# Dot products of the modulation moved from the pooling inputs to beside two merges of a mixer

## The chip, the cores and the metric

The kernel runs on one core of a Trainium2 chip. The metric is the device time of one execution in microseconds (us), as the median of several runs. A trace of one execution, the profiled one, gives the times of single instructions; they are counted from the start of its span.

## The reference

Two layers over x of 512 rows and 1024 columns. Each layer has a feed-forward network (FFN), a mixer of three branches, and a second FFN. Nine modulation vectors of a layer come from the vector c:

```python
c_act = jax.nn.silu(c)
for l in range(DEPTH):
    mod = (c_act @ w_ada[l] + b_ada[l]).reshape(B, N_MOD, D_MODEL)
    h = modulate(rms_norm(x, norm_gain[l, 0]), mod[:, 0], mod[:, 1])
    x = x + 0.5 * mod[:, 2][:, None, :] * swiglu(h, ...)
    h = modulate(rms_norm(x, norm_gain[l, 1]), mod[:, 3], mod[:, 4])
    x = x + mod[:, 5][:, None, :] * hybrid_mixer(h, ...)
    h = modulate(rms_norm(x, norm_gain[l, 2]), mod[:, 6], mod[:, 7])
    x = x + 0.5 * mod[:, 8][:, None, :] * swiglu(h, ...)
```

The mixer has attention branches a and c, and branch b, which takes trailing averages over 2, 4, 8 and 16 rows for four groups of 128 channels and maps each group by a 128x128 matrix. The three are merged:

```python
branch = jnp.einsum('bsnw,nwd->bsnd', ys, w_branch)
gates = jax.nn.sigmoid(g_lin.reshape(B, S, N_BRANCHES, D_MODEL))
merged = jnp.sum(gates * branch, axis=2)
return merged @ w_out
```

## The kernel before

Everything is held transposed, 128 channels by 512 rows, in float32. A float32 product is made of three TensorE matmuls of rounded parts: `hi` by `hi`, `lo` by `hi` and `hi` by `lo` (lines 119, 120 and 121). `wchunk` fetches a 512 KB piece of weights on SyncE's queue (L266) into one of two `raw` buffers, ScalarE copies its `whi` (L277), and VectorE subtracts it to give `wlo` (L279); there are three of each. Products collect in four PSUM buffers called `acc`.

**The dots.** `c_act @ w_ada` is done on VectorE: 144 dot products, one for each of 2 layers x 9 vectors x 8 blocks of 128. `mod_step` loads a 512 KB piece of `w_ada` (L203) into a buffer of the named tag and takes its product with `silc`, the spread-out `c_act`, with a sum per partition (L206); small instructions behind it make a scale (L215) or a half (L217). The first 16 are done at the start. The other 128 wait in `mod_queue`, in order of layer and vector. Each call of `wchunk` calls `side_work`, which adds `MOD_RATE` to a credit while `in_ffn` is set and the tag is `v2`, and takes a dot from the queue (`mod_pop`) for each whole credit. `mod_need(l, j)` takes at once all that are missing up to vector j. It is called ahead of each part's down products for the gate of that FFN, at the head of the last part's first half through `prefetch` for what the next sub-layer wants (`mod_need(l, 5)` ahead of a mixer), and before the mixer's `w_out` products. `v2` has 4 buffers, the tag `b` has 17.

**An FFN.** It goes through its hidden blocks in three parts. Each makes the gate and up products of some blocks, then the down products of these blocks in two halves of 512 output columns. In the down products `MOD_RATE` is 1.25; in gate and up it is 1.0 in part 0 and 0 in the others. The last part's two halves also start the next sub-layer: the tag is set to `raw` there, so that no dot is taken beside them other than by `mod_need`.

**A mixer.** Behind the attention of branch c, which carries the merge of branch a, `Mixer.run` loads `silc` again and the pooling matrices, and then writes out, in order:

- four pooling inputs by `pool_front`: a chunk of weights, 24 matmuls, a copy `u` on ScalarE (L1027), one to four window adds on GpSimd (L1033), three VectorE instructions for the difference (`hd` L1037, `ssum` L1039 and L1040) and a split (L384, L385). `pool_back`, put off by `later(60, ...)`, multiplies by the group's matrix (three matmuls) and makes `y` (L1050 on ScalarE, L1051 on VectorE);
- the merge of branch c: for each of 8 columns a gate (24 matmuls over a `w_ubg` chunk), a tanh (L1083), 12 matmuls by half a `w_branch` chunk, and `put_c` (L1142 on VectorE, an add on GpSimd at L1143);
- the merge of branch b in the same form, with a split of the finished column in `put_b`;
- the `w_out` products, with `residual_tail` (L434) for each column block.

In the mixer `in_ffn` is set from ahead of the pooling inputs to behind merge c, with tag `v2` and rate 1.0: 16 dots, 4 at the pooling inputs and 12 beside merge c.

A scheduler orders each engine's instructions by expected times, so the order on an engine is not that of the source line by line.

Of the kernel before, what the change touches and what calls it, by code (L numbers as in the profile page):

```python
# [15 lines left out]
F32 = mybir.dt.float32  # L16
# [6 lines left out]
P = 128  # L23
T = 512
D = 1024
# [15 lines left out]
def encoder_kernel(tc, xT, c, w_ada, b_ada, gains, w_gate, w_up, w_down, w_qkv, w_f, w_ubg,  # L41
# [16 lines left out]
    NB, NRAW = 17, 2  # L58

    def nm(s):  # L60
        uid[0] += 1
        return f"{s}_{uid[0]}"

    def st(shape, dt, tag, bufs):
        return sb.tile(shape, dt, tag=tag, bufs=bufs, name=nm(tag))
# [4 lines left out]
    def mmt(shape=(P, T)):  # L70
        return ps.tile(list(shape), F32, tag="mm", bufs=4, name=nm("mm"))
# [17 lines left out]
    class Task:  # L89
# [3 lines left out]
        def run(self):  # L93
            fn, self.fn = self.fn, None
            if fn is not None:
                fn()

    def later(delay, fn, group=None):
        t = Task(pe[0] + delay, fn, group)
        tasks.append(t)  # L100
        return t
# [85 lines left out]
    @contextlib.contextmanager  # L187
    def after(what):

        if what in last:  # L190
            with tc.issue_after(last[what]):
                yield
        else:
            yield
# [3 lines left out]
    apre = cp.tile([P, L, 3, KD], F32, name="apre")  # L198

    def mod_step(l, j, d, tag="raw"):  # L200
        raw = st([P, D], F32, tag, {"v2": 4, "raw": NRAW}[tag])
        with after("dma"):
            nc.sync.dma_start(raw, w_ada[l, j, d])  # L203
        m = modc[:, l, j, d:d + 1]
        with after("norm"):
            dot = nc.vector.tensor_tensor_reduce(out=raw, in0=raw, in1=silc[0], scale=1.0,  # L206
                                                 scalar=badac[:, l, j, d:d + 1], op0=ALU.mult, op1=ALU.add,
                                                 accum_out=m).ins
        s, kind = divmod(j, 3)
        if kind == 1:  # L210
            g = gainc[:, l, s, d:d + 1]
            if in_start[0]:
                nc.scalar.activation(apre[:, l, s, d:d + 1], m, AF.Identity, scale=g, bias=g)
                return dot
            return nc.vector.scalar_tensor_tensor(apre[:, l, s, d:d + 1], m, 1.0, g, op0=ALU.add, op1=ALU.mult).ins  # L215
        if kind == 2:
            nc.vector.tensor_scalar(m, m, 0.5, None, op0=ALU.mult)  # L217
# [6 lines left out]
    mod_tag = ["v2"]  # L224

    def mod_pop():
        if mod_ptr[0] < len(mod_queue):
            mod_step(*mod_queue[mod_ptr[0]], mod_tag[0])
            mod_ptr[0] += 1
# [5 lines left out]
    MOD_RATE = [1.0]  # L235
    in_ffn = [True]
# [14 lines left out]
    def side_work(side=True):  # L251
        if quiet[0] > 0:
            quiet[0] -= 1
            if quiet[0] == 0:
                gate.clear()
        elif side and in_ffn[0] and mod_tag[0] == "v2":
            mod_credit[0] += MOD_RATE[0]
            while mod_credit[0] >= 1.0:
                mod_credit[0] -= 1.0
                mod_pop()  # L260
# [301 lines left out]
    class Ffn:  # L562
# [32 lines left out]
        def run(self, nxt):  # L595
            l, s, ms = self.l, self.s, self.ms
            in_ffn[0] = True
            mod_tag[0] = "v2"
            parts = ((0, 6), (6, 8), (14, 8))
            for part, (f0, nf) in enumerate(parts):  # L600
                acts = []
                n = 0
                if part == 0 and self.norm is None:
                    acts = self.start()
                    n = 3
                    blocks = Blocks()
                elif part == 0:
                    g0, u0, g1 = self.pre
                    pg, pu, pg1 = mmt(), mmt(), mmt()
                    for hs in range(2):  # L610
                        self.norm.back(hs, acc if hs else mmt)
                        cols = slice(hs * HALF, (hs + 1) * HALF)
                        if hs == 0:
                            later(FRONT1, lambda: self.norm.front(1, acc))
                            later(BACK1, lambda: self.norm.back(1, acc))
                        for k in range(KD):
                            self.unit(pg, g0, cols, (k,))
                            self.unit(pu, u0, cols, (k,))
                        self.unit(pg1, g1, cols)
                    u1 = self.gate_up(1, 1)  # L620
                    acts.append(self.act(0, pg, pu))
                    pu1 = mmt()
                    self.unit(pu1, u1)
                    acts.append(self.act(1, pg1, pu1))
                    n = 2
                    blocks = Blocks(self.norm.xa, modc[:, l, 3 * ms])
                if part == 0:
                    blocks.schedule(T_FIRST, T_STEP)
                elif part == 1:
                    blocks.finish()  # L630
                MOD_RATE[0] = 0.0 if part else 1.0
                while part and n < nf:
                    both = [apply(p, AF.Silu)
                            for p in seven([w_gate[l, s, f0 + n + i] for i in range(2)], blocks, acc)]
                    ups = seven([w_up[l, s, f0 + n + i] for i in range(2)], blocks, mmt)
                    for i, sg in enumerate(both):
                        acts.append(self.act(n + i, None, ups[i], sg))
                    n += 2
                while n < nf:
                    g = self.gate_up(0, f0 + n)  # L640
                    u = self.gate_up(1, f0 + n)
                    pg, pu = mmt(), mmt()
                    self.unit(pg, g)
                    self.unit(pu, u)
                    acts.append(self.act(n, pg, pu))
                    n += 1
                mod_need(l, 3 * ms + 2)
                MOD_RATE[0] = 1.25
                for c0 in (0, T):
                    def src(c):  # L650
                        r0 = (f0 + 2 * c) * P
                        return w_down[l, s, r0:r0 + 2 * P, c0:c0 + T].rearrange("(k p) c -> p k c", p=P)

                    def ops(hi, lo, kt, j):
                        return (hi[:, j * P:(j + 1) * P], lo[:, j * P:(j + 1) * P],
                                acts[kt][:, 0, :], acts[kt][:, 1, :])

                    last = part == len(parts) - 1
                    if last and c0 == 0 and nxt is not None:
                        nxt.prefetch("v2")  # L660
                        mod_tag[0] = "raw"
                    split = last and c0 > 0
                    hook = None
                    if split:
                        hook = nxt.prefetch_weights if nxt is not None else (lambda: None)
                    for j, hs, o in k_outer(src, nf // 2, ops, hook):
                        d = c0 // P + j
                        residual_tail(d, hs, o, modc[:, l, 3 * ms + 2, d:d + 1], nxt if last else None)
                        if last and nxt is None:
                            cols = slice(0, T) if hs is None else slice(hs * HALF, (hs + 1) * HALF)  # L670
                            nc.sync.dma_start(out[:, d, cols], xd(d)[:, cols])
# [373 lines left out]
    def pool_back(l, g, b, wp, ys):  # L1045
        py = acc()
        triple(py, wp[0][:, g, :], wp[1][:, g, :], b[:, 0, :], b[:, 1, :], True, True)
        y = blk("b")
        sc = psc[:, l, g:g + 1]
        nc.scalar.activation(y[:, 0, :], py, AF.Identity, scale=sc)  # L1050
        nc.vector.scalar_tensor_tensor(y[:, 1, :], py, sc, y[:, 0, :].bitcast(F32), op0=ALU.mult, op1=ALU.subtract)  # L1051
        ys.append(y)
# [39 lines left out]
    def drain(*gens):  # L1092
        for it in gens:
            for _ in it:
                pass

    class Mixer:
# [10 lines left out]
        def run(self, nxt):  # L1108
# [53 lines left out]
            silc[0] = st([P, D], F32, "b", NB)  # L1162
            nc.sync.dma_start(silc[0], sil_dram.broadcast_to([P, D]))
            wp = wpool_load(l)
            in_ffn[0] = True
            mod_tag[0] = "v2"
            MOD_RATE[0] = 1.0
            mc = merge_units(l, 2, yc, put_c)
            for gi in range(4):
                b = pool_front(l, gi)  # L1170
                later(60, lambda gi=gi, b=b: pool_back(l, gi, b, wp, yb))
            drain(mc)
            in_ffn[0] = False
            poll(True)
            mb = merge_units(l, 1, yb, put_b)
            drain(mb)

            for b in range(4):
                xb = blk("xv", F32)
# [84 lines left out]
```

## Time and profile before

| what | value |
|---|---|
| median of 3 runs | 2412.22 us (2412.08 to 2413.41) |
| the profiled execution | 2411.93 us, its span 2410.1 us |
| its mean TensorE clock | 0.998 of full speed |
| TensorE (PE) busy | 98% |
| VectorE (DVE) busy | 72% |
| ScalarE (ACT) busy | 50% |
| GpSimd (POOL) busy | 15% |
| the dots, L206 | 144, 195.4 us in all |

In the rows of a timeline the first two numbers are the start and the length in us; then come engine, line, operation, output and inputs, and shapes. A bracket at the end gives the time for which the engine had been idle before it, and what ended that. The merge of branch c starts at about 682 us in layer 0 and 1874 us in layer 1; the last part of FFN 1 takes its first half of down products at about 320 to 340 us and 1510 to 1530 us.

### The profile page before, as it was taken

Reading aid. Unit: us, or ns where it says so; the run is one execution under the profiler, and the core shown is the slowest. Engines: PE = TensorE matmul, PEld = TensorE weight load, DVE = VectorE, ACT = ScalarE, POOL = GpSimd, SP = SyncE. Lnnn points to the kernel's source line nnn. Section 1 sums busy time; section 2 is a strip of 40 time slices with the busy share of each in tenths; the row PEclk is TensorE's granted clock in tenths of the full one; section 3 lists DMA queues with packets and bytes.
Section 4 is the critical chain, followed back from the end, with each engine's and each line's share of the span. In section 5 each row is a group of like instructions: output and inputs, shape, how many; then the busy total and the mean of one; then the engine's idle time right before and its main releaser. Section 6 shows DMA issues by size and latency. Waiting matters only on the chain. (4 is left out here: it accounts for less than half of the span.)

```text
span 2410.1 us, 36817 instructions
## 1 busy us (share of the span) xinstructions
PE 2363.2 (98%) x14106; PEld 2088.6 (87%) x14106; DVE 1729.5 (72%) x3070; ACT 1199.8 (50%) x2090; POOL 353.3 (15%) x423
## 2 busy tenths in 40 slices
PE   7999999999999999999999999999999999999999
PEld 5898998778878898989998989978787788989898
DVE  8987876787673377878577878677866734769583
ACT  5353545786632353535553636466865233536362
POOL 3000011144432110000000000102444322000000
PEclk9999999999999999999999999999999999999999
DMA  7635352323353425353325352523234533333233
GB/s 273 210 106 193 106 201 80 93 79 108 116 196 131 140 97 205 103 190 106 132 82 194 103 183 105 201 79 98 79 116 142 183 114 140 130 107 104 92 106 103
DMA packets 116437, 320.93 MB, mean 133 GB/s; under 512 B 11139, under 2 KB 13315, under 8 KB 116261
## 3 DMA queue, kind: packets, MB, share of 16 engines
q1 hardware_dynamic: 115106, 314.38, 38.6%
q0 software_dynamic: 1152, 4.19, 0.4%
q8 instruction: 111, 1.82, 0.3%
q14 instruction: 66, 0.53, 0.1%
q10 hardware_dynamic: 2, 0.00, 0.0%
HBM read 312.16 MB, written 6.38 MB: 132 GB/s over the span
## 5 line engine op out<-in xcount | busy, mean ns | idle before, releaser
L277 ACT CAST whi<-raw 128x1024 fp32r<-128x1024 f32 (+1 forms) x267 | 277.4, 1043 | 449.1 <-PE acc L120 258.6
L279 DVE TENSOR_TENSOR wlo<-raw,whi 128x1024 fp32r<-128x1024 f32 x259 | 323.5, 1252 | 208.4 <-ACT whi L277 205.7
L119 PE MATMUL acc<-b,whi 128*128 128x512 f32 (+1 forms) x960 | 360.6, 376 | 0.0
L120 PE MATMUL acc<-b,whi 128*128 128x512 f32 (+1 forms) x960 | 357.1, 372 | 0.0
L121 PE MATMUL acc<-b,wlo 128*128 128x512 f32 (+1 forms) x960 | 356.6, 371 | 0.0
L206 DVE CUSTOM_DVE_ANT_0 v<-v,b,badac 128x1024 f32<-128x1024 f32 x144 | 195.4, 1365 | 40.2 <-DMA v<-in_w_ada_dram 40.1
L119 PEld LDWEIGHTS acc<-b,whi 128*128 128x128 f32 x960 | 180.8, 188 | 31.4
L121 PEld LDWEIGHTS acc<-b,wlo 128*128 128x128 f32 x960 | 180.8, 188 | 31.3
L120 PEld LDWEIGHTS acc<-b,whi 128*128 128x128 f32 x960 | 180.9, 188 | 29.9
L121 PE MATMUL acc<-hhi,wlo 128*128 128x512 f32 x480 | 189.4, 395 | 7.9 <-DVE wlo L279 7.9
L119 PE MATMUL acc<-hhi,whi 128*128 128x512 f32 x480 | 192.2, 402 | 4.0 <-ACT whi L277 2.3
L120 PE MATMUL acc<-hlo,whi 128*128 128x512 f32 x480 | 189.5, 395 | 0.7 <-DVE hlo L711 0.7
L385 DVE TENSOR_TENSOR ptb<-v,ptb 128x1024 fp32r<-128x1024 f32 x128 | 156.6, 1224 | 35.7 <-ACT ptb L384 34.3
L384 ACT CAST ptb<-v 128x1024 fp32r<-128x1024 f32 x128 | 134.0, 1050 | 93.0 <-DVE v L452 46.4
L384 ACT CAST whi<-raw 128x1024 fp32r<-128x1024 f32 (+1 forms) x128 | 106.8, 834 | 97.9 <-PE acc L120 50.3
L119 PE MATMUL acc<-whi,hhi 128*128 128x512 f32 x336 | 137.8, 411 | 0.9 <-DVE xv L385 0.9
L121 PE MATMUL acc<-whi,hlo 128*128 128x512 f32 x336 | 132.0, 393 | 0.0
L120 PE MATMUL acc<-wlo,hhi 128*128 128x512 f32 x336 | 131.7, 392 | 0.0
L385 DVE TENSOR_TENSOR wlo<-raw,whi 128x1024 fp32r<-128x1024 f32 (+1 forms) x128 | 121.9, 952 | 7.0 <-ACT whi L384 5.2
L121 PEld LDWEIGHTS acc<-hhi,wlo 128*128 128x128 f32 x480 | 91.4, 190 | 29.0 <-DVE wlo L279 9.8
L434 DVE SCALAR_TENSOR_TENSOR xv<-acc,modc,xv 128x512 f32<-128x512 f32 (+1 forms) x112 | 76.9, 690 | 50.0 <-PE acc L121 50.0
L329 POOL TENSOR_TENSOR ssum<-ssum,t 128x256 f32<-128x256 f32 (+1 forms) x45 | 46.7, 1037 | 445.7 <-ACT t L328 445.6
(314 smaller groups left out, 6606.0 us busy)
## 6 DMA issues: line engine op xcount, KB each, us to landing
v<-in_w_ada_dram SPq DMA_DIRECT2D x144, 512.0 KB, 4.8
raw<-in_w_down_dram SPq DMA_DIRECT2D x88, 512.0 KB, 3.7
raw<-in_w_up_dram SPq DMA_DIRECT2D x82, 512.0 KB, 3.7
raw<-in_w_gate_dram SPq DMA_DIRECT2D x79, 512.0 KB, 3.7
raw<-in_w_ubg_dram SPq DMA_DIRECT2D x56, 512.0 KB, 3.5
raw<-in_w_qkv_dram SPq DMA_DIRECT2D x42, 512.0 KB, 3.9
raw<-in_w_branch_dram SPq DMA_DIRECT2D x24, 512.0 KB, 3.8
raw<-in_w_out_dram SPq DMA_DIRECT2D x16, 512.0 KB, 3.6
```

The source lines that it names most:

```text
L119: mm(o, lh, rh, start=start, stop=False)
L120: mm(o, lh, rl, start=False, stop=False)
L121: mm(o, ll, rh, start=False, stop=stop)
L206: dot = nc.vector.tensor_tensor_reduce(out=raw, in0=raw, in1=silc[0], scale=1.0, scalar=badac[:, l, j, d:d + 1], op0=ALU.mult, op1=ALU.add ...
L277: nc.scalar.copy(hi, raw)
L279: lo_eng.tensor_tensor(lo, raw, hi.bitcast(F32), op=ALU.subtract)
L329: nc.gpsimd.tensor_tensor(self.ssum[:, cols], self.ssum[:, cols], q, op=ALU.add)
L384: nc.scalar.copy(hi, src)
L385: nc.vector.tensor_tensor(lo, src, hi.bitcast(F32), op=ALU.subtract)
L434: nc.vector.scalar_tensor_tensor(x, acc_j, gate, x, op0=ALU.mult, op1=ALU.add)
```

## The change

The setting of `in_ffn`, tag and rate moves in `Mixer.run` from ahead of the pooling inputs to behind them, and it is taken back behind the merge of branch b instead of between the two merges. The tag in between is `b`, not `v2`, and for that `mod_step` learns the tag `b` and `side_work` lets every tag pass but `raw`. Behind the mixer the tag goes back to `raw`. The rate beside the down products falls from 1.25 to 1.0.

A mixer so takes 24 dots instead of 16: none at the pooling inputs, 12 beside merge c, and 12 at merge b, of which 8 are spread over its columns and 4 stand next to the start of `w_out`. The number of all dots stays 144; fewer are left for the down products.

```diff
     def mod_step(l, j, d, tag="raw"):
-        raw = st([P, D], F32, tag, {"v2": 4, "raw": NRAW}[tag])
+        raw = st([P, D], F32, tag, {"v2": 4, "raw": NRAW, "b": NB}[tag])
...
-        elif side and in_ffn[0] and mod_tag[0] == "v2":
+        elif side and in_ffn[0] and mod_tag[0] != "raw":
             mod_credit[0] += MOD_RATE[0]
...
                 mod_need(l, 3 * ms + 2)
-                MOD_RATE[0] = 1.25
+                MOD_RATE[0] = 1.0
...
             wp = wpool_load(l)
-            in_ffn[0] = True
-            mod_tag[0] = "v2"
-            MOD_RATE[0] = 1.0
             mc = merge_units(l, 2, yc, put_c)
             for gi in range(4):
                 b = pool_front(l, gi)
                 later(60, lambda gi=gi, b=b: pool_back(l, gi, b, wp, yb))
+            in_ffn[0], mod_tag[0], MOD_RATE[0] = True, "b", 1.0
             drain(mc)
-            in_ffn[0] = False
             poll(True)
             mb = merge_units(l, 1, yb, put_b)
             drain(mb)
+            in_ffn[0], mod_tag[0] = False, "raw"
```

## The prediction

> **What bounds the kernel now.** I read the page's engine line first, then the table by stretches around the pooling inputs, then the timelines of TensorE and of its feeders there.
>
> ```profile
> PE 2363.2 (98%) x14106; PEld 2088.6 (87%) x14106; DVE 1729.5 (72%) x3070; ACT 1199.8 (50%) x2090; POOL 353.3 (15%) x423
> ```
>
> PE is busy 2363.2 of 2410.1 us, so the change can pay only where PE stands still or runs slowly. The table by stretches (span, then busy time and count of PE, PEld, DVE, ACT, POOL, then granted clock, DMA share, GB/s) has two such places, the same one in each layer:
>
> ```profile
> 682.00:686.50 4.50, 0.55 (x4) 0.13 (x2) 3.55 (x7) 1.10 (x2) 2.64 (x6) 0.86 0.60 233
> 686.50:692.00 5.50, 5.50 (x13) 4.34 (x14) 5.50 (x6) 1.64 (x3) 4.26 (x4) 0.50 0.54 191
> 692.00:700.00 8.00, 8.00 (x36) 6.55 (x36) 7.49 (x14) 2.65 (x4) 2.86 (x3) 0.99 0.41 135
> 1878.70:1884.00 5.30, 5.28 (x16) 4.19 (x17) 5.30 (x6) 1.67 (x3) 4.04 (x4) 0.68 0.60 198
> ```
>
> A PE that looks full from 686.5 to 692 starts 13 matmuls where the next stretch starts 36 in 8.00 us. TensorE's timeline names the cause:
>
> ```profile
> 660.15 0.63 PE L966 MATMUL mm<-ident,t 128*128 128x128 f32 x4 [1.29 <-DVE t L954]
> ...
> 660.85 0.39 PE L121 MATMUL acc<-hhi,wlo 128*128 128x512 f32 x1
> ...
> 682.16 0.39 PE L120 MATMUL acc<-hlo,whi 128*128 128x512 f32 x1
> 686.50 0.80 PE L121 MATMUL acc<-hhi,wlo 128*128 128x512 f32 x1 [3.95 <-DVE wlo L279]
> ...
> 692.16 0.40 PE L119 MATMUL acc<-hhi,whi 128*128 128x512 f32 x1
> ...
> 698.36 0.39 PE L119 MATMUL acc<-hhi,whi 128*128 128x512 f32 x1
> ...
> 1874.43 0.39 PE L120 MATMUL acc<-hlo,whi 128*128 128x512 f32 x1
> 1878.72 0.50 PE L121 MATMUL acc<-hhi,wlo 128*128 128x512 f32 x1 [3.91 <-DVE wlo L279]
> ```
>
> Gate 0 of the merge of branch c has its `whi`, but waits 3.95 and 3.91 us for its `wlo`. Then the clock is down. In layer 0 it is 0.50, and 13 matmuls need 692.16 - 686.50 = 5.66 us; at 8.00/36 = 0.222 us each they would take 2.9, so 2.8 are lost. In layer 1 (clock 0.68) 16 matmuls fill 5.30 us, which is worth 1.7. The two places cost 3.95 + 2.8 + 3.91 + 1.7 = **12.4 us**, the most that the pooling part can give.
>
> Beside it stands a rule of the Trainium skill, page "TensorE: Matmul & The Clock Gate", section "Part 1: The HAM clock gate": an idle window of about 3.4 us halves the clock, and about 3.4 us of activity restore it. The trace agrees: the gaps of 3.95 and 3.91 us were followed by clocks of 0.50 and 0.68, the 1.29 us gap at 660.15 by a matmul of 0.39 us, as long as any at full speed, and 5.66 us passed before full speed came back. By that rule a remaining wait under 3.4 us costs its own length alone.
>
> **Pooling inputs.** Dots stand ahead of that `wlo` on DVE; these are the last three, and what else is in its queue:
>
> ```profile
> 674.94 2.06 DVE L206 CUSTOM_DVE_ANT_0 v<-v,b,badac 128x1024 f32<-128x1024 f32 x1
> ...
> 677.69 1.27 DVE L206 CUSTOM_DVE_ANT_0 v<-v,b,badac 128x1024 f32<-128x1024 f32 x1
> ...
> 681.48 2.06 DVE L206 CUSTOM_DVE_ANT_0 v<-v,b,badac 128x1024 f32<-128x1024 f32 x1
> ...
> 684.46 0.18 DVE L1037 TENSOR_TENSOR hd<-strip,icnt 128x16 f32<-128x16 f32 x1 [0.92 <-POOL strip L1033]
> ...
> 685.23 1.22 DVE L279 TENSOR_TENSOR wlo<-raw,whi 128x1024 fp32r<-128x1024 f32 x1
> ...
> 693.70 0.74 DVE L1051 SCALAR_TENSOR_TENSOR b<-acc,psc,b 128x512 fp32r<-128x512 f32 x1
> ```
>
> The change takes them out, and in the changed kernel's order this `wlo` also stands ahead of the third input's `hd`, `ssum` chain. So the last three dots (2.06 + 1.27 + 2.06 = 5.39) and the wait of 0.92 go: ready at 685.23 + 1.22 - 6.31 = 680.1, where PE wants it at 682.4. This wait is cured with 2 us to spare, without counting the earlier ones.
>
> What is late next? Gate 1's first matmul (698.36 now, 698.36 - 3.95 - 2.8 = 691.6 without the stall) needs the PSUM buffer of the second pool product, which `y1`'s L1051 (693.70 now) releases. In the new order that L1051 stands behind the fourth input's `hd` chain, and so behind POOL's four window adds. POOL and the ACT copies that start it:
>
> ```profile
> 678.38 0.58 ACT L1027 COPY b<-acc 128x512 f32<-128x512 f32 x1
> ...
> 686.87 0.58 ACT L1027 COPY b<-acc 128x512 f32<-128x512 f32 x1
> ...
> 679.04 1.43 POOL L1033 TENSOR_TENSOR strip<-b 128x512 f32<-128x512 f32 x1 [1.19 <-ACT b L1027]
> ...
> 680.55 1.90 POOL L1033 TENSOR_TENSOR strip<-strip 128x512 f32<-128x512 f32 x1
> ...
> 682.58 1.85 POOL L1033 TENSOR_TENSOR strip<-strip 128x512 f32<-128x512 f32 x1
> ...
> 687.60 1.13 POOL L1033 TENSOR_TENSOR strip<-b 128x512 f32<-128x512 f32 x1 [2.16 <-ACT b L1027]
> ...
> 692.81 2.11 POOL L1033 TENSOR_TENSOR strip<-strip 128x512 f32<-128x512 f32 x1
> ```
>
> The fourth copy (686.87) comes behind the third input's chain. That is shorter by its adds, 684.43 - 679.04 = 5.39 against three at 1.13, so 2.0, and by the dot of 2.06 that held the second input's `hd`, less about 1.05 for gate 0's `whi`, which moves ahead of the third copy: some 3.0 together. So the copy ends at 684.4; the four adds take 694.92 - 687.60 = 7.3 as traced beside dots, 4 x 1.13 = 4.5 alone; the `hd` chain 685.23 - 684.46 = 0.8 and L1051 0.74 follow. End: 690.4 to 693.3 against 691.6, a wait of 0 to 1.7. In the new order two dots still stand ahead of that chain, so I take 1.3. If the copy gains 0.8 only, it is 3.9. **Gain 12.4 - 2 x 1.3 = 9.8 us**, bounds 12.4 and about 4.
>
> **Down products.** With 1.0 for 1.25 they carry fewer dots, so that the forced batch ahead of the last half of part 2 of FFN 1 (`mod_need(l, 5)`) grows from 7 to some 10. Its loads pass the weights on SP's queue:
>
> ```profile
> 318.64 12.40 SPq L203 DMA_DIRECT2D v<-in_w_ada_dram  x7
> 331.15 0.89 SPq L266 DMA_DIRECT2D raw<-in_w_down_dram  x2
> ...
> 337.52 1.05 ACT L277 CAST whi<-raw 128x1024 fp32r<-128x1024 f32 x1 [4.90 <-DMA raw<-in_w_down_dram]
> ...
> 334.46 1.27 DVE L206 CUSTOM_DVE_ANT_0 v<-v,b,badac 128x1024 f32<-128x1024 f32 x1
> ...
> 338.60 1.23 DVE L279 TENSOR_TENSOR wlo<-raw,whi 128x1024 fp32r<-128x1024 f32 x1 [1.58 <-ACT whi L277]
> ...
> 340.26 0.39 PE L119 MATMUL acc<-b,whi 128*128 128x512 f32 x1
> ```
>
> Four `v2` buffers hold the loads back to the pace of the dots. Three more put the first weight's issue behind the end of the fifth dot, the one ahead of 334.46, so at about 334.3 instead of 331.15. Where it was cast 6.4 us after issue, it lands 4.5 to 7 us after; `whi` (1.05) and `wlo` (1.23) follow at 341.1 to 343.6, where PE takes `whi` at 340.26 and `wlo` 0.5 later. Waits of 0.4 to 2.9, softened because the scheduler has put `whi` products of two accumulators ahead: I take 1.2 a layer, **2.4 us**, bounds 0 and 6. The lower rate gains nothing elsewhere, as PE has no idle time in the down products; FFN 2 of layer 1 loses its last 8 dots to the mixer for nothing.
>
> **Merges.** A merge with dots is traced: c, today.
>
> ```profile
> 715.38 0.42 SPq L203 DMA_DIRECT2D v<-in_w_ada_dram  x1
> ...
> 719.90 1.28 DVE L206 CUSTOM_DVE_ANT_0 v<-v,b,badac 128x1024 f32<-128x1024 f32 x1 [2.35 <-DMA v<-in_w_ada_dram]
> ...
> 720.82 1.05 ACT L277 CAST whi<-raw 128x1024 fp32r<-128x1024 f32 x1 [6.61 <-PE acc L120]
> ...
> 721.91 1.23 DVE L279 TENSOR_TENSOR wlo<-raw,whi 128x1024 fp32r<-128x1024 f32 x1 [0.51 <-ACT whi L277]
> ...
> 724.02 0.39 PE L121 MATMUL acc<-hhi,wlo 128*128 128x512 f32 x1
> ```
>
> Of every two columns one gate has a dot ahead of its `wlo`. This `wlo` ends at 723.14, 0.9 before PE wants it, and the dot ends 0.7 before the `wlo` starts: a load may take 4.5 + 0.7 + 0.9 = 6.1 us before PE waits. The table by line and tile gives all loads and dots:
>
> ```profile
> L206 DVE CUSTOM_DVE_ANT_0 v<-v,b,badac x144: 1269/1280/2630, 11.4 to 2113.0; 128x1024 f32<-128x1024 f32 x144
> DMA to landing us min/median/max: 3.4/4.8/8.1
> ```
>
> At the median 4.8 nothing waits, and the 8 spread dots beside merge b, like the 4 bunched next to `w_out`, are hidden by its columns (24 matmuls for the gate and 12 for the branch, at 0.222 us: 16 us per pair). Merge b has its own split on DVE and POOL adds that may stretch a dot to 2.06, which eats 0.8 of the 1.6 to spare. I take 0.5 us for both layers, bounds 0 and 24 (the first rival).
>
> Sum: 9.8 - 2.4 - 0.5 = 6.9. 2411.93 for the profiled execution, which stands 0.3 under the runs' median of 2412.22 and 1.8 over its span, gives **2405.0**.
>
> **Rivals.** *Slower:* loads of the dots land late in the merges. Twelve even gates (six a mixer) have a dot ahead; each costs landing time less 6.1. At 8.1, the longest traced, that is 12 x 2.0 = 24, so 2405.0 + 24 = 2429; from a mean landing of 6.8 on the change is slower than before. For it: up to three transfers of 128x1024 f32 per column of 8 us, and many loads issued in a row behind the pooling. Against it: the row above, at the same pace. *Same:* the wait moves to gate 1. If the fourth copy gains only 0.8, both layers wait 3.9 and lose the clock too (2.8, 1.7), and nothing is left of the 12.4: 2411.9 + 2.4 less 12.4 - 2 x 3.9 - 2.8 - 1.7 = 0.1, about 2414. For it: POOL's adds in a row and dots beside them. Beside it, the page "SBUF — State Buffer", section "Who interferes with whom", says that a DVE instruction with two SBUF inputs and a GpSimd one that reads SBUF exclude each other; the dots of 1.27 and 2.06 and the adds of 1.13 and 1.90 agree; by it the chain would keep its 7.3 wherever the two dots fall among the adds, and gate 1 would wait 1.7 rather than 1.3. *Better:* POOL runs its adds near 1.13 and the batch is covered by the `whi` products: 2411.9 - 12.4 = 2399.5.
>
> **How the numbers follow.** 0.2% (4.8 us) is about what a measurement tells from no change: 2407.4 to 2417.0 is "same". Forecast 0.46; better 0.11; wait at gate 1 or a batch of 3 us and more a layer 0.25; late loads 0.18. The forecast's own spread is 2401 to 2409; the top of it lies in "same", the bottom of the third case in "faster", which I set against each other. Faster 0.57, same 0.25, slower 0.18. The range reaches from 2399 to 2416.
>
> **What would show it.** Right: no gap over 2 us before gate 0's L121 at 682 and 1874, clock 1.0 there, gate 1's first L119 released by L1051 at most 2 us late, a gap near 1 us in the second half of part 2 of FFN 1, merge b without PE gaps. Wrong: PE gaps before even gates' L121 in the merges with DVE at `wlo` behind a dot that waited for its load; a clock under 1 behind gate 1; or gaps over 3 us near 340 and 1530.

## The result and the profile after

The changed kernel takes 2407.35 us (median of 11 runs, 2402.77 to 2410.06) against 2411.89 us (11 runs, 2410.91 to 2413.41). The ratio is 0.9978, 95% interval 0.9970 to 0.9987: a gain of 4.5 us. 2405.0 was forecast, with a range of 2399 to 2416. The profiled execution took 2409.17 us (span 2407.4), 2.8 less than that of before.

**Gate 0 no longer waits.** The table by stretches of the changed kernel, with the columns of before; the next rows follow from its TensorE and VectorE timelines and those of the two helpers:

```profile
682.00:686.50 4.50, 4.50 (x22) 3.69 (x21) 2.25 (x5) 2.01 (x3) 2.27 (x6) 1.00 0.92 350
692.00:700.00 8.00, 6.46 (x29) 4.96 (x28) 5.50 (x9) 2.65 (x4) 2.81 (x4) 1.00 0.12 33
```

```profile
695.72 0.49 PE L119 MATMUL acc<-hhi,whi 128*128 128x512 f32 x1 [1.54 <-DVE b L1051]
...
1884.45 0.51 PE L119 MATMUL acc<-hhi,whi 128*128 128x512 f32 x1 [1.57 <-DVE b L1051]
```

```profile
679.66 1.23 DVE L279 TENSOR_TENSOR wlo<-raw,whi 128x1024 fp32r<-128x1024 f32 x1 [0.26 <-ACT whi L277]
...
687.78 2.06 DVE L206 CUSTOM_DVE_ANT_0 b<-b,b,badac 128x1024 f32<-128x1024 f32 x1
...
689.77 2.05 DVE L206 CUSTOM_DVE_ANT_0 b<-b,b,badac 128x1024 f32<-128x1024 f32 x1
...
694.16 0.18 DVE L1037 TENSOR_TENSOR hd<-strip,icnt 128x16 f32<-128x16 f32 x1 [2.33 <-POOL strip L1033]
...
694.92 0.74 DVE L1051 SCALAR_TENSOR_TENSOR b<-acc,psc,b 128x512 fp32r<-128x512 f32 x1
```

```profile
686.51 0.57 ACT L1027 COPY b<-acc 128x512 f32<-128x512 f32 x1
...
687.23 1.53 POOL L1033 TENSOR_TENSOR strip<-b 128x512 f32<-128x512 f32 x1 [2.20 <-ACT b L1027]
...
692.84 1.28 POOL L1033 TENSOR_TENSOR strip<-strip 128x512 f32<-128x512 f32 x1
```

From 682.0 to 686.5, where 4 matmuls started, 22 do, at full clock. The `wlo` of gate 0 ends at 680.89. What is late next is what the prediction named: gate 1, released by `y1`'s L1051, which stands behind the fourth input's `hd`, which waits for POOL's fourth add (to 694.12), with two dots ahead of it. Gate 1 waits 1.54 and 1.57 us. The four adds took 694.12 - 687.23 = 6.9 us beside those dots, close to the 7.3 of before and far from the 4.5 that four adds of 1.13 would take.

**The forced batch costs more than was forecast.** SyncE, ScalarE and TensorE around the last part of FFN 1 in layer 0, then TensorE in layer 1:

```profile
318.10 15.54 SPq L203 DMA_DIRECT2D v<-in_w_ada_dram  x9
333.69 0.43 SPq L266 DMA_DIRECT2D raw<-in_w_down_dram  x1
335.18 0.33 SPq L203 DMA_DIRECT2D v<-in_w_ada_dram  x1
...
340.26 1.04 ACT L277 CAST whi<-raw 128x1024 fp32r<-128x1024 f32 x1 [8.25 <-DMA raw<-in_w_down_dram]
```

```profile
341.36 0.50 PE L119 MATMUL acc<-b,whi 128*128 128x512 f32 x1 [1.44 <-ACT whi L277]
...
342.62 0.50 PE L121 MATMUL acc<-b,wlo 128*128 128x512 f32 x1 [0.30 <-DVE wlo L279]
...
1529.63 0.50 PE L119 MATMUL acc<-b,whi 128*128 128x512 f32 x1 [2.33 <-ACT whi L277]
...
1530.89 0.74 PE L121 MATMUL acc<-b,wlo 128*128 128x512 f32 x1 [0.30 <-DVE wlo L279]
```

```profile
339.73:343.13 3.40, 1.66 (x6) 0.96 (x6) 2.44 (x6) 1.27 (x2) 0.00 (x0) 1.00 0.96 374
343.14:346.55 3.41, 3.41 (x9) 2.67 (x9) 3.19 (x5) 1.86 (x2) 0.00 (x0) 0.50 0.75 247
1527.56:1530.97 3.41, 1.04 (x4) 0.57 (x4) 2.40 (x6) 1.04 (x1) 0.00 (x0) 1.00 0.82 317
1530.98:1534.38 3.40, 3.40 (x8) 2.67 (x9) 3.37 (x5) 2.09 (x2) 0.00 (x0) 0.50 0.64 196
```

The weight that was issued at 331.15 now is at 333.69, behind nine loads of dots. PE waits 1.44 + 0.30 us in layer 0 and 2.33 + 0.30 in layer 1, and behind the wait, in both places, the granted clock is 0.50 for 3.41 us. PE is busy all through these stretches, so half of them is lost: 1.7 us more each.

**Merge b carries its dots for nothing.** Two stretches that lie within merge b, one in each layer, after and then before:

```profile
757.00:818.00 61.00, 61.00 (x271) 50.52 (x270) 32.72 (x48) 19.87 (x26) 12.47 (x8) 1.00 0.54 185
1946.00:2008.00 62.00, 62.00 (x275) 51.36 (x274) 33.53 (x48) 19.88 (x26) 12.62 (x8) 1.00 0.53 184
```

```profile
757.00:818.00 61.00, 61.00 (x271) 50.52 (x270) 23.60 (x26) 18.56 (x25) 14.34 (x8) 1.00 0.39 129
1946.00:2008.00 62.00, 62.00 (x275) 51.35 (x274) 24.37 (x26) 20.00 (x27) 14.50 (x8) 1.00 0.37 128
```

VectorE has 9.1 and 9.2 us more to do and the traffic rises from 129 to 185 GB/s in layer 0. TensorE stays full and has the same 271 and 275 matmuls. In merge c of layer 1 one gate waits 0.32 us for its `wlo` (at 1910.72), which it did not before. The longest load of a dot takes 6.6 us to land, against 8.1 before, and the median load 4.9 against 4.8:

```profile
DMA to landing us min/median/max: 3.4/4.9/6.6
```

### The profile page after: what moved, and what is told of

Same layout as the page of the kernel before. It is cut to its first block, busy times and chain, and to the rows that moved or that the text cites. A ratio compares the mean times of both kernels' runs of the same rounds, so it can differ in the third digit from the quotient of the medians.

```text
span 2407.4 us, 36815 instructions
## 1 busy us (share of the span) xinstructions
PE 2361.9 (98%) x14106; PEld 2086.8 (87%) x14106; DVE 1728.9 (72%) x3070; ACT 1197.8 (50%) x2090; POOL 351.7 (15%) x423
## 5 line engine op out<-in xcount | busy, mean ns | idle before, releaser
L206 DVE CUSTOM_DVE_ANT_0 v<-v,b,badac 128x1024 f32<-128x1024 f32 x96 | 127.2, 1333 | 12.3 <-DMA v<-in_w_ada_dram 12.0
L119 PEld LDWEIGHTS acc<-hhi,whi 128*128 128x128 f32 x480 | 90.7, 189 | 26.1 <-DVE b L1051 4.0
```

The source lines that it names most:

```text
L119: mm(o, lh, rh, start=start, stop=False)
```

## The experiments

Each ran beside the kernel before on one chip: e1 to e4 on one, e5 to e8 on a second, e9 and e10 on a third. The time of before there was 2411.86, 2413.03 and 2412.87 us, and gains are taken against these.

Gains by stage, below, come from the two profiled executions: the k-th matmul start of one trace is set against the k-th of the other (each has 14106, in almost the same order). From the pooling inputs into merge b (655 to 760 us of the kernel before, and 1848 to 1950) the changed kernel gains 4.8 and 3.7 us; in the last part of FFN 1 it loses 2.7 and 3.1; in the last FFN it loses 1.7.

**e1 to e4: where the gain comes from and where it goes.**

e1, the rate alone set back:

```diff
-                MOD_RATE[0] = 1.0
+                MOD_RATE[0] = 1.25
```

> The changed kernel with 1.25 instead of 1.0 beside the down products, so that the forced batch ahead of the last half of FFN 1 is 7 dots in layer 0 and 5 in layer 1 again; the mixer keeps its 24. Theory: the pooling part gains 10.3 us and the batch of 10 costs 5.8 (excess of PE over full pace 3.62 - 0.88 and 4.61 - 1.54). So 2411.9 - 10.3, about 2402, no PE gap over 1 us near 340 and 1525, and the 1.5 us gap at gate 1 stays. Rival, what is lost is lost to the dots beside merge b: the time stays at 2407.

2402.60 us, ratio 0.9968 (0.9956 to 0.9979). No gap near 340 and 1525 is left, and gate 1 waits as in the changed kernel:

```profile
693.05 0.50 PE L119 MATMUL acc<-hhi,whi 128*128 128x512 f32 x1 [1.57 <-DVE b L1051]
```

So with the old rate the change gains 9.3 us, and the lower rate takes half of it. The rival, dots beside merge b as the cost, falls. By stage, e1 gains 8.9 us from the pooling inputs into merge b and 3.0 in the last part of FFN 1, where layer 1 now forces five dots and before seven, and loses 1.7 in the last FFN.

e2, the kernel before with the rate alone changed:

```diff
-                MOD_RATE[0] = 1.25
+                MOD_RATE[0] = 1.0
```

> The kernel before with 1.0 for 1.25 alone: the forced batch is 9 dots, pooling inputs and merges as before. Theory: the batch costs 4 to 6 us, so 2416 to 2418, with gaps of 1 to 2.5 us in the last part of FFN 1 of both layers. Rival (the batch is covered, the loss lies in the mixer): 2412.

2415.82 us, ratio 1.0018 (1.0010 to 1.0027): 4.0 us slower by the rate alone. TensorE's timeline shows both the gap in the batch and the old one at gate 0:

```profile
341.39 0.50 PE L119 MATMUL acc<-b,whi 128*128 128x512 f32 x1 [1.43 <-ACT whi L277]
...
688.97 0.79 PE L121 MATMUL acc<-hhi,wlo 128*128 128x512 f32 x1 [3.94 <-DVE wlo L279]
...
1533.88 0.50 PE L119 MATMUL acc<-b,whi 128*128 128x512 f32 x1 [1.58 <-ACT whi L277]
```

e3, the changed kernel with a short batch:

```diff
         def prefetch(self, xtag):
-            mod_need(self.l, 5)
+            mod_need(self.l, 4)
```

> The changed kernel, but the prefetch of a mixer asks for its shift and scale alone (4 instead of 5): the forced batch is 2 dots, and the 8 of the mixer's gate come first among the dots beside its merges. Theory: without the batch the 5.8 us come back, 2407.4 - 5.8, about 2401.5, no PE gap near 340 and 1525. Rival (the batch costs nothing, or the dots that are now missing from FFN 1 cost as much elsewhere): 2407.

2400.87 us, ratio 0.9955 (0.9942 to 0.9967), 11.0 us under before and 6.5 under the change by the medians. TensorE is full in both places:

```profile
310.00:355.00 45.00, 45.00 (x293) 41.24 (x293) 30.72 (x43) 23.71 (x36) 6.24 (x5) 1.00 0.52 168
1500.00:1540.00 40.00, 40.00 (x251) 36.24 (x250) 24.78 (x33) 20.47 (x30) 6.08 (x5) 1.00 0.59 195
```

The mixer's gate needs its eight dots only ahead of `w_out`, and the 24 dots beside the merges deliver them in time. e1, e2 and e3 agree: the batch is the cost of the lower rate.

e4, the four pooling inputs in the other order, with `yb` still in the order of the groups:

```diff
-            for gi in range(4):
+            for gi in (3, 2, 1, 0):
...
-        ys.append(y)
+        ys.insert(0, y)
```

> The changed kernel with the four pooling inputs taken from the widest window to the narrowest, so that the last of them has one window add and not four. Theory: gate 1's wait of 1.55 and 1.57 us stands behind POOL's four adds (y1's L1051 is queued behind that chain on DVE), so it goes: 2407.4 - 3.1, about 2404.3. Rival A, the two dots ahead of that chain hold it by their loads: the gap stays, 2407. Rival B, the wide window now delays the first inputs and gate 0 waits again: 2409 or more.

2412.79 us, ratio 1.0004 (0.9995 to 1.0013). A miss: the gain is gone. The four adds at the start delay each later input, since each copy stands on ScalarE behind the split of the input ahead, and in the new order two dots stand between the last `hd` chain and `y1`'s L1051. VectorE and TensorE there:

```profile
691.69 1.28 DVE L206 CUSTOM_DVE_ANT_0 b<-b,b,badac 128x1024 f32<-128x1024 f32 x1
...
692.89 1.28 DVE L206 CUSTOM_DVE_ANT_0 b<-b,b,badac 128x1024 f32<-128x1024 f32 x1
...
694.70 0.74 DVE L1051 SCALAR_TENSOR_TENSOR b<-acc,psc,b 128x512 fp32r<-128x512 f32 x1
```

```profile
695.50 0.63 PE L119 MATMUL acc<-hhi,whi 128*128 128x512 f32 x1 [2.40 <-DVE b L1051]
```

Gate 1 waits 2.40, not 0, and in layer 0 the clock drops behind it. Neither rival was this: gate 0 waits only 0.31 in layer 0. The run says nothing for or against POOL's adds as the cause of gate 1's wait, since it put dots in their place.

**e7 and e8: gate 1's wait.** e7 is e3 with the pool products in another PSUM group:

```diff
     def pool_back(l, g, b, wp, ys):
-        py = acc()
+        py = mmt()
```

> The changed kernel with the short forced batch and the pool products (pool_back) in the other group of PSUM buffers, mm, so that gate 1 no longer needs the buffer that y1's L1051 releases. Theory: the gaps of 1.69 and 1.69 us at gate 1 go, 2400.9 - 3.4, about 2397.5. Rival (gate 1 is late for another reason that ends just ahead of it, its weights or the tanh of gate 0): the gap stays over 1 us, 2400.

2398.26 us, ratio 0.9944 (0.9930 to 0.9957). Gate 1 starts without a gap, on TensorE's timeline:

```profile
689.48 0.39 PE L119 MATMUL acc<-hhi,whi 128*128 128x512 f32 x1
...
716.07 0.50 PE L121 MATMUL acc<-hhi,wlo 128*128 128x512 f32 x1 [0.76 <-DVE wlo L279]
```

So it was the PSUM buffer, and the clock shows no loss there. A gap of 0.76 us appears at 716.07, in merge c, behind a dot whose load came late. The intervals of e3 and e7 overlap, and e7's profiled execution is not the faster one (2398.17 against 2397.79). The 2.4 us that it gains over e3 by stage, from the pooling inputs into merge b, it gives back in new waits behind, such as 0.76 us at 846.13. So e7 shows what gate 1 waited for, and not a faster kernel than e3.

e8 is e7 with 1.25 for 1.0:

> As the last one, with 1.25 for 1.0 beside the down products: no forced batch at all in FFN 1. Theory (the rate matters only through the batch): the same time as the last one, about 2397.5. Rival (1.25 itself crowds the down products): over 2 us slower.

2399.88 us, ratio 0.9942 (0.9930 to 0.9955), the same as e7: without the batch the rate does not matter. Both are faster than the kernel before and the changed kernel.

**e5, e9 and e10: the place or the buffer.** e5 moves the dots out of the pooling inputs and changes nothing else: the three settings stand behind the loop, with `v2` as before.

```diff
-            in_ffn[0] = True
-            mod_tag[0] = "v2"
-            MOD_RATE[0] = 1.0
...
+            in_ffn[0], mod_tag[0], MOD_RATE[0] = True, "v2", 1.0
             drain(mc)
```

> The kernel before with the dots taken out of the pooling inputs alone: 12 dots beside merge c, none beside merge b, 1.25 beside the down products; the 4 that are missing are forced beside w_out. Theory (the pooling part gains 10.3 us, dots beside merge b cost and gain nothing): 2411.9 - 10.3, about 2402 as with the 24 dots and 1.25 (2402.6); at most 2 us more if the 4 forced dots delay w_out. Rival (the 12 dots beside merge b carry part of the gain, or cost part of it): over 2 us away from 2402.6.

2413.47 us, ratio 1.0003 (0.9994 to 1.0012): no gain at all, against 2402 expected. VectorE and TensorE show why:

```profile
682.58 2.06 DVE L206 CUSTOM_DVE_ANT_0 v<-v,b,badac 128x1024 f32<-128x1024 f32 x1
...
703.72 1.28 DVE L206 CUSTOM_DVE_ANT_0 v<-v,b,badac 128x1024 f32<-128x1024 f32 x1 [2.68 <-DMA v<-in_w_ada_dram]
...
705.59 1.22 DVE L279 TENSOR_TENSOR wlo<-raw,whi 128x1024 fp32r<-128x1024 f32 x1
```

```profile
706.86 0.50 PE L121 MATMUL acc<-hhi,wlo 128*128 128x512 f32 x1 [2.89 <-DVE wlo L279]
```

With `v2` the scheduler still draws dots into the pooling inputs, like that at 682.58. Gate 0 no longer waits; the stall has moved to gate 2, whose `wlo` waits behind a dot that waits for its load. This is the prediction's *slower* rival in small: one even gate a layer, 2.89 and 2.61 us.

e9 is e5 with the tag `b`, for which `mod_step` and `side_work` have the lines of the change:

```diff
-            in_ffn[0], mod_tag[0], MOD_RATE[0] = True, "v2", 1.0
+            in_ffn[0], mod_tag[0], MOD_RATE[0] = True, "b", 1.0
             drain(mc)
+            mod_tag[0] = "raw"
             in_ffn[0] = False
```

> As e5 (the kernel before, dots only out of the pooling inputs, 12 beside merge c, 1.25 beside the down products), but with the dots' buffers of tag b and not v2; the 4 missing dots fall near the end of merge b. In the order of instructions no dot stands ahead of gate 1's wlo now, where e5 has four. Theory A, the buffers decide where the scheduler puts the dots, and that made the gain: 2411.9 - 10.3, about 2402, gate 0 without a wait. Theory B, e5 lost its gain to having too few dots in the mixer (4 forced beside w_out): 2412 as e5.

2407.30 us, ratio 0.9974 (0.9963 to 0.9985). The wait at gate 0 is gone and gate 1's is that of the changed kernel, 1.53 us, as A has it. By stage it gains 9.0 us from the pooling inputs into merge b, as e1 does, but 5.6 in all. In the stretch from 705 to 820, where the 4 missing dots stand bunched near merge b's end (805 to 814, and in the two `raw` buffers of the weights, since the tag is `raw` there), TensorE starts 6 matmuls fewer than in e1 (e9, then e1), which is 1.4 us:

```profile
705.00:820.00 115.00, 114.27 (x503) 94.01 (x502) 55.84 (x74) 32.41 (x41) 26.27 (x15) 1.00 0.44 143
```

```profile
705.00:820.00 115.00, 115.00 (x509) 95.23 (x508) 68.12 (x97) 33.59 (x43) 27.10 (x15) 1.00 0.54 188
```

Layer 1 loses as much there, and the second FFNs lose 1.2 and 1.0 us, which stays open.

e10 is the kernel before with another tag in the mixer alone, and the same two lines for it:

```diff
             in_ffn[0] = True
-            mod_tag[0] = "v2"
+            mod_tag[0] = "b"
             MOD_RATE[0] = 1.0
...
             drain(mc)
-            in_ffn[0] = False
+            in_ffn[0], mod_tag[0] = False, "raw"
```

> The kernel before with the tag b for v2 in the mixer and nothing else: 16 dots from the pooling inputs on, 1.25 beside the down products. In its order four dots stand in the first two pooling inputs and none from there to gate 1's wlo. Theory A (buffers): gate 0's wait of 3.95 and 3.91 us goes as in the changed kernel, 2402 to 2405. Theory B (what counts is that no dot is asked for at the pooling inputs): the early dots hold up DVE and POOL as before, 2412.

2407.95 us, ratio 0.9980 (0.9971 to 0.9989): 4.9 us by a buffer's name. The dots are still asked for from the pooling inputs on, but the early ones are done ahead of the inputs' `hd` chains (the first `hd` is at 669.86), and the next stand behind gate 1's `wlo` (685.74). VectorE, with the last early dot and the next one:

```profile
664.09 1.28 DVE L206 CUSTOM_DVE_ANT_0 b<-b,b,badac 128x1024 f32<-128x1024 f32 x1
...
686.88 2.06 DVE L206 CUSTOM_DVE_ANT_0 b<-b,b,badac 128x1024 f32<-128x1024 f32 x1
```

Gate 0 does not wait. What is left is gate 1:

```profile
694.80 0.50 PE L119 MATMUL acc<-hhi,whi 128*128 128x512 f32 x1 [2.15 <-DVE b L1051]
```

By stage it gains 5.0 us from the pooling inputs into merge b, over half of the 9.0 that e9 has with the place changed too. So the tag decides whether gate 0 is cured, and B falls. Whether it is the number of buffers (17 against 4) or what else shares them, no run separates.

**e6: how much room the merges have.** e3 with two dots for each chunk:

```diff
-            in_ffn[0], mod_tag[0], MOD_RATE[0] = True, "b", 1.0
+            in_ffn[0], mod_tag[0], MOD_RATE[0] = True, "b", 2.0
```

> The changed kernel with the short forced batch (4 instead of 5 in the prefetch of a mixer) and two dots instead of one for each chunk beside the merges, 48 a mixer as far as the queue reaches. It asks how much room the merges have. Three loads of dots instead of 1.5 fall on a column of 8.2 us, beside 1.5 of weights, 4.5 x 0.5 MB in 8.2 us or 288 GB/s. Theory (a load may land 6.1 us after issue before an even gate waits): loads land later than that, some 18 even gates wait 1 to 2 us, so 2400.9 + 18 to 36, 2419 to 2437, with PE gaps ahead of L119 or L121 in the merges. Rival (the merges are far from their limit): 2401.

2411.28 us, ratio 0.9993 (0.9985 to 1.0002), some 9 us more than e3 and far less than the 18 to 36 expected. TensorE, then the loads of the dots:

```profile
693.46 0.49 PE L119 MATMUL acc<-hhi,whi 128*128 128x512 f32 x1 [3.05 <-ACT t L1083]
...
723.25 0.50 PE L121 MATMUL acc<-hhi,wlo 128*128 128x512 f32 x1 [1.31 <-DVE wlo L279]
```

```profile
DMA to landing us min/median/max: 3.4/5.5/9.7
```

Loads do land later (5.5 against 4.9 us in the changed kernel), but only one gate in a layer waits for its `wlo`, 1.31 us in layer 0 and 2.02 in layer 1. The larger part is gate 1, 3.05 and 3.06 us with a slow clock behind it. It waits there for the tanh of gate 0, which ends at 693.41 and stands on ScalarE behind the fourth input's split, and not for `y1`'s L1051: that comes only at 694.37, behind four dots. Why the order changed so was not followed up. Beside that the merges take twice the dots for one wait a layer.

## Why the prediction was right, and where it was off

**Pooling inputs.** 9.8 us forecast: 12.4 less 2 x 1.3. The gaps that are left, 1.54 and 1.57, make it 12.4 - 3.1 = 9.3. By stage it is 8.5 us, and 8.9 in e1. That e1's whole gain is also 9.3 is chance, since it holds a gain in FFN 1 and a loss in the last FFN too. The cured wait, the next late one and its cause came as worked out, and e7 shows that the cause is the PSUM buffer. For the size the prediction took 1.3 and named 1.7 for adds that keep their 7.3 us beside the dots; they took 6.9, and the wait lies between the two. The fourth copy ended at 687.45 before and ends at 687.08 now, but the waits of the batch have shifted all of the mixer: the first pool product stood at 678.49 and stands at 680.95. Against that shift of 2.5 the copy gained 2.8, where 3.0 was worked out.

**Why the pooling inputs were cured.** Here the working was incomplete. It read the new order and did not ask what made it. e5, e9 and e10 show that the tag `b` does. With the four `v2` buffers dots stand among the pooling inputs even when they are asked for behind them (e5, from 667.82 to 682.58). With `b` they stand behind gate 1's `wlo` when asked for behind the inputs (e9), and are done early when asked for ahead (e10). How the scheduler comes to this is not shown.

**Down products.** This is the term that was mis-sized: 2.4 forecast, bounds 0 and 6. The issue of the weight (334.3 forecast, 333.69 measured) and the landing (4.5 to 7 us; 6.6) were right. The waits are 1.7 and 2.6 where 1.2 was taken, and the clock took 1.7 more each: 7.7 us. Waits of before at two later places went, which I had not counted:

```profile
361.83 0.39 PE L121 MATMUL mm<-b,wlo 128*128 128x256 f32 x1 [0.76 <-DVE wlo L279]
...
1550.77 0.39 PE L119 MATMUL mm<-b,whi 128*128 128x256 f32 x1 [0.36 <-ACT whi L277]
1552.03 0.39 PE L121 MATMUL mm<-b,wlo 128*128 128x256 f32 x1 [0.76 <-DVE wlo L279]
```

That leaves 7.7 - 1.9 = 5.8, as by stage (2.7 + 3.1). e2 has the same ten loads in each layer, nine ahead of the weight and one behind, and gave 4.0: in layer 1 it waits 1.58 + 0.30 and the clock stays up. The step that failed is the clock behind these waits, which the sum puts at nothing. Beside it the prediction had read out of the Trainium skill, page "TensorE: Matmul & The Clock Gate", section "Part 1: The HAM clock gate", that a remaining wait under 3.4 us costs its own length alone. The runs show in its place that waits of 1.74 and 2.63 us cost 1.7 us of clock each. The waits themselves were also under-sized, by 2.0 us together. By stage the 2.8 us between the profiled executions are 8.5 - 5.8 - 1.7 and 1.8 in small steps elsewhere. The 1.7 are lost in the last FFN, where the order of instructions is the same; waits of 0.65 and 0.42 us there are part of it, and their cause is open.

**Merges.** 0.5 forecast, 0.3 measured, in merge c: in merge b TensorE is busy 61.00 of 61.00 and 62.00 of 62.00 us. The *slower* rival needed loads that land late twelve times; the longest took 6.6 us in the changed kernel, against 8.1 before. e6 shows that its price was too high: with loads up to 9.7 us it still met one gate a layer. In e5 it did happen, with `v2`, at gate 2 of each layer.

**The sign** held, as the interval ends at 0.9987. But 2407.35 lies on the edge of what the prediction called "faster": its bound of 2407.4 came from a median of 2412.22, and 0.2% under the 2411.89 of eleven runs would be 2407.1. Of the terms, pooling gave 0.5 to 1.3 us less, the batch cost 3.4 more and the merges 0.2 less; the medians lie 2.4 above the forecast. That they lie so near is partly luck: the batch alone was 3.4 off.

## What to carry to other kernels

When side work is moved out of a stretch, look at what makes the scheduler place it: here another pool of buffers alone gained 4.9 us, and another place in the source alone gained nothing (e5); only with the new pool did the place count. A forced batch on a queue that also carries weights is a cost to be sized first: asking for the eight dots when they are needed, not when the next stage starts, was worth more than the change itself. And follow the next late wait to the one buffer that it needs; the other PSUM group removed it with one word, though other waits then took its place.

## What the runs showed of the hardware

The clock fell after shorter waits than expected. Behind the start and outside the attention, single gaps of TensorE up to 1.7 us never slowed the matmuls behind them in these twelve traces; of ten between 2.0 and 3.1 us five did (2.01, 2.12, 2.15, 2.39 and 2.89 did not; 2.02, 2.40, 2.61, 3.05 and 3.06 did); all four of 3.9 us and more did. Of six gaps with a second one of 0.30 us close behind, those of 1.43, 1.44, 1.76 and 2.33 did, and those of 1.54 and 1.58 did not. So the length of a gap alone does not decide.

The granted clock shows what does. In each trace every change of it lies a whole multiple of 3.413 us behind its first rise, to within 0.01 us. In the changed kernel it is at half from 343.14 to 346.55 and from 1530.98 to 1534.39, and these starts are 348 steps apart. So a trace can be cut into windows of 3.413 us. Here are two neighbours of e5 and two of e6, with the columns of before (PE's busy time is the first behind the span, the granted clock the third from the end):

```profile
702.32:705.73 3.41, 1.65 (x8) 1.03 (x6) 2.01 (x4) 1.05 (x1) 0.10 (x1) 1.00 0.19 76
705.74:709.15 3.41, 2.29 (x10) 1.88 (x11) 2.80 (x3) 0.00 (x0) 1.67 (x1) 1.00 0.35 52
```

```profile
1909.37:1912.78 3.41, 1.45 (x7) 0.87 (x5) 3.41 (x9) 0.66 (x1) 1.18 (x1) 1.00 0.92 306
1912.78:1916.19 3.41, 3.36 (x8) 2.68 (x9) 3.41 (x5) 0.39 (x1) 1.14 (x1) 0.50 0.82 296
```

The gap of 2.89 us in e5 falls into two windows, which are idle for 1.76 and 1.12 us, and the clock stays. The gap of 2.02 in e6 lies almost whole in one, idle for 1.96, and the next window has half the clock. Over all windows at full clock in the twelve traces, each of the 11 with 1.96 us or more of idle TensorE was followed by one at half clock, and none with 1.69 or less was. Of five between, two were (1.73 and 1.74) and three were not (1.74, 1.76 and 1.90). So the clock fell here when TensorE was idle for a little over half of one window; the ends of matmuls are modelled, which may blur the five. The same section of the Trainium skill says that the window is free-running, and the fixed steps agree with that.

A window at half clock costs 1.7 us when TensorE is busy all through it. Before, layer 0 had two of them (685.26 to 692.08), as the wait for gate 0 still took 1.24 us of the first, and layer 1 had one. That is why the same wait lost 2.8 us of clock in one layer and 1.7 in the other. The 5.66 us that the prediction took for the time until full speed came back were the rest of those two windows. The first rise stands at another place in each of the twelve executions (25.1 to 27.5 us), so whether a wait near 2 us costs the 1.7 looks like chance. This may be part of the spread of the changed kernel's runs, which no run here tests.
